# Two columns of padding between blocks of 128 activations, and weight tiles 64 bytes further on

## The chip, the cores and the metric

The kernel runs on one core of a Trainium2 chip. The metric is device time in microseconds (us) of one execution. Engines are named as in the profile: PE is the matrix engine's matmuls, PEld its weight loads, DVE, ACT and POOL the vector, scalar and general engines, SP the queue that issues most DMAs. On-chip memory (SBUF) has 128 partitions; an address below is a byte address within a partition, and every tile stands at the same address in all partitions.

## The reference

Two layers of a decoder trunk on 256 tokens and 2048 features in float32, batch 1. Layer 0 is a gated linear recurrence (HGRN2), layer 1 a sparse attention with compressed, selected and windowed keys (NSA). Each layer projects its input with one wide matrix, mixes along the tokens, gates, projects back and normalizes:

```
q, f_logit, v, z = split(x @ w_in, 4)                      # layer 0: 2048 -> 8192
o = recurrence(q, f_logit, v); o = rms(o) * g_norm * silu(z)
h = LayerNorm(alpha * x + o @ w_out)
q, k_c, v_c, k_s, v_s, k_w, v_w, gate, z = split(h @ w_in) # layer 1: 2048 -> 7216
o = gate0*compressed + gate1*selected + gate2*windowed; o = o * silu(z)
y = LayerNorm(alpha * h + o @ w_out)
```

The matrices hold about 42 million numbers, and all of them are read once; the products with them are most of the matmuls.

## The kernel before

**Precision.** Matmul operands are of the type fp32r, a rounded float32. To keep accuracy each operand is split into a rounded part and the rest (`split`, lines 86 and 87: ACT writes the high part, DVE the low part), and each product is three matmuls: high by high, high by low, low by high.

**Activations** lie in SBUF as a `Pair`: for each group of 4 feature blocks (KG = 4 groups) a tile `hi` and a tile `lo` of 128 partitions x (4 feature blocks, 256 tokens), 4096 bytes a partition. Pair "a" is the input of a layer (tiles `ah`, `al`), Pair "b" the mixer's output (`bh`, `bl`). They come from the pool `acts`, four slots for each of the four names. `put` writes one block of 128 tokens, `at(k, c)` gives the columns c of feature block k. Each 128 x 128 block is 512 bytes a partition.

**Weights** come in tiles of 256 rows by 512 columns (`wr`, loaded by SP on line 113), are split into `wh` and `wl`, and used at once. The pool `wts` has 5 slots of each part, and a pool `wide` gives three more during layer 0.

**Two forms of the projection.** `project` (lines 153 to 155, through `tok_step`) keeps one activation block of 128 tokens stationary in the array and streams 512 weight columns: the moving operand is the weights, 512 columns a matmul (280 in the two calls that take the gate along). In order of k and then of the token tile t, three matmuls follow one another for each block. `project_t` (lines 208, 210, 211) keeps 128 weight columns stationary and streams the 256 tokens: the moving operand is the activations, 256 columns a matmul, and 12 matmuls follow for each k. `project_by_tile` is `project` one token tile after the other; the last projection's weights lie in tiles of their own (pool `late`, `summed`), so that sums of some columns can stand beside them.

**Other matmuls** are the recurrence's (lines 409 to 479), the attention's (lines 571 to 573, 796 to 813), transposes (221) and the compression of keys and values (621 and 622), where the stationary operand is a 122-column slice of `flat` (488 bytes from one slice to the next) and the moving one 256 columns of a weight tile.

**Order.** A planner orders each engine's instructions at build time; on the chip each engine follows its own list and waits on semaphores. Loads of weights are queued on SP and wait for a free slot.

**Addresses.** Pools with `side="right"` grow down from the top of SBUF, the others up from the bottom. `room(p, n)` takes n bytes to move what follows. In this kernel every block of `ah`, `al`, `bh` and `bl` begins at an address that is 64 modulo 512, and every weight slice at 320 modulo 512 (in the last projection some slices at 64). The slices of `flat` begin at all 64 multiples of 8 modulo 512.

Of the kernel before, what the change touches and what calls it, by code (L numbers as in the profile page):

```python
# [9 lines left out]
F32R = mybir.dt.float32r  # L10
# [8 lines left out]
S = 256  # L19
NT = S // 128  # L20
KT = D // 128
KG = KT // 4
# [33 lines left out]
def trunk(ctx, tc, a, out):  # L56
# [6 lines left out]
    consts = ctx.enter_context(tc.tile_pool(name="consts", bufs=1))  # L63
    acts = ctx.enter_context(tc.tile_pool(name="acts", bufs=4))


    def room(p, n):

        p.tile([128, n // 4], F32, name=f"room{n}")

    room(ctx.enter_context(tc.tile_pool(name="edge", bufs=1, side="right")), 160)
    wts = ctx.enter_context(tc.tile_pool(name="wts", bufs=5, side="right"))
    pj = ctx.enter_context(tc.tile_pool(name="pj", bufs=4, space=PSUM))
    mx = ctx.enter_context(tc.tile_pool(name="mx", bufs=4, space=PSUM))
# [3 lines left out]
    def pjb(shape):  # L78
        return pj.tile(shape, F32, name="pjb", tag="pjb")

    def mxb(shape):
        return mx.tile(shape, F32, name="mxb", tag="mxb")

    def split(hi, lo, src):

        act.activation(hi, src, AF.Copy)  # L86
        dve.tensor_tensor(lo, src, hi.bitcast(F32), op=OP.subtract)  # L87
# [8 lines left out]
    class Pair:  # L96


        def __init__(self, name):
            self.hi = [acts.tile([128, 4, S], F32R, name=name + "h") for _ in range(KG)]  # L100
            self.lo = [acts.tile([128, 4, S], F32R, name=name + "l") for _ in range(KG)]

        def put(self, g, t, src):
            c = slice(128 * t, 128 * (t + 1))
            split(self.hi[g][:, :, c], self.lo[g][:, :, c], src)

        def at(self, k, c):
            return self.hi[k // 4][:, k % 4, c], self.lo[k // 4][:, k % 4, c]

    def load(w, j, c0, n):  # L110

# [4 lines left out]
    def weights(w, j, c0, n):  # L116
        return parts(load(w, j, c0, n))
# [16 lines left out]
    def slot(shape, dtype, name, n, more):  # L134

        turn[name] = i = (turn.get(name, -1) + 1) % (n + more)
        p, b = (extra[0], more) if extra[0] and i >= n else (wts, n)
        if spare[0] and name == "wr" and extra[0] is None:

            spare[1] = i = (spare[1] + 1) % (n + SPARE)  # L140
            p, name, b = (spare[0], "ws", SPARE) if i >= n else (wts, name, n)
        return p.tile(shape, dtype, name=name, tag=name, bufs=b)
# [6 lines left out]
        return hi, lo  # L149

    def tok_step(ps, xs, k, t, wh, wl):
        xh, xl = xs.at(k, slice(128 * t, 128 * (t + 1)))
        pe.matmul(ps, xh, wh, start=(k == 0), stop=False)  # L153
        pe.matmul(ps, xh, wl, start=False, stop=False)  # L154
        pe.matmul(ps, xl, wh, start=False, stop=(k == KT - 1))  # L155

    def project(xs, w, c0, also=None, n=512):

        ps = [pjb([128, n]) for _ in range(NT)]
        for j in range(KT // 2):  # L160
            hi, lo = weights(w, j, c0, n)
            for kk in range(2):
                for t in range(NT):
                    tok_step(ps[t], xs, 2 * j + kk, t, hi[:, kk], lo[:, kk])
            if also:
                also(j)
        return ps
# [28 lines left out]
    def project_t(xs, w, c0, before=None, also=None):  # L196

        ps = [pjb([128, 2, S]) for _ in range(2)]
        for j in range(KT // 2):
            hi, lo = before(j) if before else weights(w, j, c0, 512)  # L200
            for kk in range(2):
                k = 2 * j + kk
                xh, xl = xs.at(k, slice(0, S))
                for b in range(4):
                    o = ps[b // 2][:, b % 2]
                    c = slice(128 * b, 128 * (b + 1))

                    pe.matmul(o, hi[:, kk, c], xh, start=(k == 0 and b % 2 == 0), stop=False,  # L208
                              skip_group_check=True)
                    pe.matmul(o, hi[:, kk, c], xl, start=False, stop=False, skip_group_check=True)  # L210
                    pe.matmul(o, lo[:, kk, c], xh, start=False, stop=(k == KT - 1),  # L211
                              skip_group_check=True)
            if also:
                also(j)
        return ps
# [122 lines left out]
    with tc.tile_pool(name="start", bufs=4) as start:  # L338

        idle = start.tile([128, 128], F32, name="idle", bufs=1)  # L340
        dve.memset(idle, 0.0)
        ps = mxb([128, 128])
        for _ in range(WARM):
            pe.matmul(ps, idle, idle, start=True, stop=True)
        loaded = {}

        def fetch(j):
            xr = start.tile([128, 2, S], F32, name="xr")
            raw = slot([128, 2, 512], F32, "wr", 3, 1)
            for c in (slice(0, 1), slice(1, 2)) if j < 2 else (slice(0, 2),):  # L350
                nc.sync.dma_start(xr[:, c], xt[:, 2 * j:2 * j + 2][:, c])
                nc.sync.dma_start(raw[:, c], w0[256 * j:256 * (j + 1), D:D + 512].rearrange(
                    "(k p) n -> p k n", p=128)[:, c])
            loaded[j] = xr, raw

        def before(j):
            if j == 0:
                fetch(0)
                fetch(1)
            if j + 2 < KT // 2:  # L360
                fetch(j + 2)
            xr, raw = loaded.pop(j)
            hi, lo = slot([128, 2, 512], F32R, "wh", 5, 3), slot([128, 2, 512], F32R, "wl", 5, 3)
            xh, xl = (v[j // 2][:, 2 * (j % 2):2 * (j % 2) + 2] for v in (xT.hi, xT.lo))
            for c in (slice(0, 1), slice(1, 2)) if j < 2 else (slice(0, 2),):
                split(xh[:, c], xl[:, c], xr[:, c])
                split(hi[:, c], lo[:, c], raw[:, c])
            return hi, lo

        forget = project_t(xT, w0, D, before=before)  # L370

    with tc.tile_pool(name="setup", bufs=1) as setup:
# [119 lines left out]
    with tc.tile_pool(name="m0", bufs=1) as m0:  # L492
        ad = m0.tile([128, NT, 4, 128], F32, name="ad")
        pool.memset(ad, 0.0)
        for g in range(4):
# [5 lines left out]
            v = m0.tile([128, NT, 512], F32, name="v")  # L501
# [25 lines left out]
    with tc.tile_pool(name="n0", bufs=2) as n0:  # L527
        hb = n0.tile([128, NT, D], F32, name="hb", bufs=1)
        stats = n0.tile([128, NT, 4, 6], F32, name="stats", bufs=1)
        for c in range(4):  # L530
            cs = slice(512 * c, 512 * (c + 1))
            xr = n0.tile([128, NT, 512], F32, name="xr")
# [33 lines left out]
    def split2(pair, at, src):  # L566
        split(pair[0][at], pair[1][at], src)
# [77 lines left out]
    with tc.tile_pool(name="cmp", bufs=1) as cp:  # L645
# [57 lines left out]
        h = ck.hidden()  # L703
        ps = mxb([128, 4, NB])
# [9 lines left out]
        n = (512 + 48) // 2  # L714
        for t, ps in enumerate(project(hT, w1, C_VW, step, n=n)):
            split2(vals, (slice(None), t, 1, slice(0, n)), ps)
        h = cv.hidden()
# [5 lines left out]
        ps = mxb([128, 4, 128])  # L723
# [4 lines left out]
        ps = ps.rearrange("p g d -> p (g d)")  # L728
        for i in range(2):
            r, o = (slice(64 * b, 64 * b + 64) for b in (i, 1 - i))  # L730
            l = slice(64 * i + 32, 64 * i + 64)
# [9 lines left out]
    at = attention.enter_context(tc.tile_pool(name="at", bufs=2))  # L741
# [77 lines left out]
    def query(g):  # L819
        pq = project(hT, w1, C_Q + 512 * g)  # L820
        q = [rotary(at, t, pq[t]) for t in range(NT)]
        ps = [scores(g, t, q[t]) for t in range(NT)]
        return [values(g, t, ps[t]) for t in range(NT)]
# [41 lines left out]
    def summed(raw):  # L865


        parts = [late.tile([128, 2, 576], F32R, name=name) for name in ("wh", "wl")]
        ws = n1.tile([128, 2], F32, name="ws")
        with tc.high_priority(AHEAD):  # L870
            split(*(bass.AP(tensor=v.tensor, offset=v.offset, ap=[v.ap[0], [576, 2], [320, 2], [1, 256]])
                    for v in parts), raw.rearrange("p k (u n) -> p k u n", u=2))
            dve.tensor_reduce(ws, raw[:, :, 256:512], axis=AX.X, op=OP.add)
            split(*(v[:, :, 256:258] for v in parts), ws[:, :, None].to_broadcast([128, 2, 2]))

        def halves(v, kk):
            return bass.AP(tensor=v.tensor, offset=v.offset + 576 * kk, ap=[v.ap[0], [320, 2], [1, 256]])

        return [[halves(v, kk) for v in parts] + [v[:, kk, 0:258] for v in parts] +
                [v[:, kk, 320:576] for v in parts] for kk in range(2)]  # L880

    for c in range(4):
        cs = slice(512 * c, 512 * (c + 1))

        xr = []
# [51 lines left out]
        if c < 3:  # L937
            for t, ps in enumerate(project(oT, a["l1_w_out"], 512 * c, behind)):
                residual(t, ps)
            if c == 2:  # L940
                last_xr = fetch(3)
            if c == 1:
                late = ctx.enter_context(tc.tile_pool(name="late", bufs=8, side="right"))
                g1, b1 = row("l1_ln_g"), row("l1_ln_b")
        else:
            xr.append(last_xr)
            project_by_tile(oT, a["l1_w_out"], 512 * c, finish, summed=summed)
# [33 lines left out]
```

## Time and profile before

| | |
|---|---|
| median of 3 runs | 999.18 us (998.26 to 1000.69) |
| the profiled execution's own time | 999.29 us |
| its span, first to last instruction | 997.6 us |
| PE busy | 981.8 us (98%), 6041 matmuls |
| DVE, ACT, POOL busy | 683.2, 545.4, 116.2 us |
| mean granted PE clock | 0.995 of 2.4 GHz |

A matmul's duration in the profile is its way through the array, and matmuls overlap; what they cost in a stream is the time from one start to the next. That is called the spacing below, and is read from the timeline (starts in us) or from a window's count.

### The profile page before, as it was taken

The numbers are of one execution on the slowest core, as the hardware profiler recorded it, in microseconds if no ns is written. First come the engines' busy times: TensorE is split into PE (matmuls) and PEld (weight loads), VectorE is DVE, ScalarE is ACT, GpSimd is POOL, SyncE is SP. The second block draws the span as 40 slices with busy tenths as digits, with TensorE's granted clock in tenths as the row PEclk, the third lists the DMA queues.
The fourth block names the chain that finished last, engine by engine and source line by source line (L and its number), as shares of the span: only waits on it lengthen the run. The fifth ranks groups of instructions, "written<-read, shape, count | busy, mean of one in ns | idle before, by whom it ended". The sixth has DMA issues, their size and how long they took to land.

```text
span 997.6 us, 15935 instructions
## 1 busy us (share of the span) xinstructions
PE 981.8 (98%) x6041; PEld 882.6 (88%) x6041; DVE 683.2 (68%) x1123; ACT 545.4 (55%) x872; POOL 116.2 (12%) x180
## 2 busy tenths in 40 slices
PE   9999999999999999999999999999999999998996
PEld 8988998899889988888889888999989889986885
DVE  6796668666775677646576756555858568786677
ACT  6654455445544554434476655555857667765340
POOL 0400300030002000310011020101020022042200
PEclk9999999999999999999999999999999999999998
DMA  9775466556555565558467776566454455486662
GB/s 306 258 228 165 150 182 175 167 156 186 173 168 160 173 182 160 167 167 273 147 232 226 244 229 213 174 211 189 125 170 128 148 151 164 151 240 204 202 199 84
DMA packets 101068, 185.25 MB, mean 186 GB/s; under 512 B 6128, under 2 KB 20544, under 8 KB 100736
## 3 DMA queue, kind: packets, MB, share of 16 engines
q1 hardware_dynamic: 99520, 178.67, 57.6%
q0 software_dynamic: 1472, 5.56, 1.7%
q8 instruction: 47, 0.77, 0.3%
q14 instruction: 29, 0.24, 0.1%
HBM read 180.02 MB, written 4.19 MB: 185 GB/s over the span
## 4 chain that ended last, share of the span: by engine, by line
PE 87%; DVE 5%; DMA 4%; ACT 2%; issue 1%; SPq 1%; POOL 0%; DVEq 0%; ACTq 0%; POOLq 0%
PE pjb L154 16%; PE pjb L155 16%; PE pjb L153 16%; PE pjb L208 9%; PE pjb L211 9%; PE pjb L210 9%; DMA wr<-in_l_w_out_dram 3%; DVE wl L87 3%; PE mxb L448 2%; PE mxb L221 1%; ACT wh L86 1%; PE mxb L571 1%; PE mxb L572 1%; PE mxb L573 1%; PE mxb L804 1%
## 5 line engine op out<-in xcount | busy, mean ns | idle before, releaser
L87 DVE TENSOR_TENSOR wl<-wr,wh 128x1024 fp32r<-128x1024 f32 (+2 forms) x305 | 372.0, 1225 | 180.4 <-ACT wh L86 178.8
L86 ACT ACTIVATE wh<-wr 128x1024 fp32r<-128x1024 f32 (+2 forms) x305 | 316.9, 1044 | 304.8 <-PE pjb L155 152.9
L208 PE MATMUL pjb<-ah,wh 128*128 128x256 f32 x832 | 236.8, 285 | 0.5 <-ACT wh L86 0.5
L210 PE MATMUL pjb<-al,wh 128*128 128x256 f32 x832 | 236.2, 285 | 0.0
L211 PE MATMUL pjb<-ah,wl 128*128 128x256 f32 x832 | 235.3, 285 | 0.5 <-DVE wl L87 0.5
L154 PE MATMUL pjb<-wl,ah 128*128 128x512 f32 (+1 forms) x576 | 219.4, 381 | 0.0
L153 PE MATMUL pjb<-wh,ah 128*128 128x512 f32 (+1 forms) x576 | 219.0, 381 | 0.0
L155 PE MATMUL pjb<-wh,al 128*128 128x512 f32 (+1 forms) x576 | 218.9, 380 | 0.0
L208 PEld LDWEIGHTS pjb<-ah,wh 128*128 128x128 f32 x832 | 159.4, 192 | 1.3 <-ACT wh L86 0.9
L211 PEld LDWEIGHTS pjb<-ah,wl 128*128 128x128 f32 x832 | 158.9, 192 | 1.0 <-DVE wl L87 0.9
L210 PEld LDWEIGHTS pjb<-al,wh 128*128 128x128 f32 x832 | 159.3, 192 | 0.4
L155 PEld LDWEIGHTS pjb<-wh,al 128*128 128x128 f32 x576 | 108.3, 188 | 19.6
L153 PEld LDWEIGHTS pjb<-wh,ah 128*128 128x128 f32 x576 | 108.2, 188 | 19.3
L154 PEld LDWEIGHTS pjb<-wl,ah 128*128 128x128 f32 x576 | 108.3, 188 | 18.7
L154 PE MATMUL pjb<-wl,bh 128*128 128x512 f32 (+2 forms) x272 | 103.7, 381 | 1.1 <-DVE wl L87 1.1
L153 PE MATMUL pjb<-wh,bh 128*128 128x512 f32 (+2 forms) x272 | 103.5, 381 | 1.0 <-ACT wh L86 1.0
L155 PE MATMUL pjb<-wh,bl 128*128 128x512 f32 (+2 forms) x272 | 103.4, 380 | 0.0
L154 PEld LDWEIGHTS pjb<-wl,bh 128*128 128x128 f32 x272 | 51.6, 190 | 11.0 <-DVE wl L87 1.7
L153 PEld LDWEIGHTS pjb<-wh,bh 128*128 128x128 f32 x272 | 51.6, 190 | 10.9 <-ACT wh L86 1.4
L155 PEld LDWEIGHTS pjb<-wh,bl 128*128 128x128 f32 x272 | 51.6, 190 | 9.5
L511 POOL TENSOR_TENSOR gz<-gz,gn 128x512 f32<-128x512 f32 x8 | 13.6, 1700 | 312.3 <-ACT gz L510 311.7
L87 DVE TENSOR_TENSOR wl<-ws,wh 128x1024 fp32r<-128x1024 f32 (+2 forms) x33 | 28.2, 863 | 18.4 <-ACT wh L86 18.3
(229 smaller groups left out, 1060.5 us busy)
## 6 DMA issues: line engine op xcount, KB each, us to landing
wr<-in_l_w_in_dram SPq DMA_DIRECT2D x218, 512.0 KB, 3.8
wr<-in_l_w_out_dram SPq DMA_DIRECT2D x64, 512.0 KB, 4.5
ws<-in_l_w_in_dram SPq DMA_DIRECT2D x12, 512.0 KB, 4.5
wr<-in_l_cmp_w_k_dram SPq DMA_DIRECT2D x5, 512.0 KB, 3.9
wr<-in_l_cmp_w_v_dram SPq DMA_DIRECT2D x5, 512.0 KB, 3.8
wr<-in_l_w_in_dram SPq DMA_DIRECT2D x9, 280.0 KB, 3.2
xr<-in_x_dram POOLq DMA_DIRECT2D x4, 512.0 KB, 5.7
norm<-hb POOLq DMA_DIRECT2D x2, 1024.0 KB, 5.7
```

Source lines behind the costliest of these rows:

```text
L86: act.activation(hi, src, AF.Copy)
L87: dve.tensor_tensor(lo, src, hi.bitcast(F32), op=OP.subtract)
L153: pe.matmul(ps, xh, wh, start=(k == 0), stop=False)
L154: pe.matmul(ps, xh, wl, start=False, stop=False)
L155: pe.matmul(ps, xl, wh, start=False, stop=(k == KT - 1))
L208: pe.matmul(o, hi[:, kk, c], xh, start=(k == 0 and b % 2 == 0), stop=False, skip_group_check=True)
L210: pe.matmul(o, hi[:, kk, c], xl, start=False, stop=False, skip_group_check=True)
L211: pe.matmul(o, lo[:, kk, c], xh, start=False, stop=(k == KT - 1), skip_group_check=True)
L221: last[0] = pe.transpose(ps[:, i], src[:, i], ident).ins
L448: pe.matmul(ps[:, h], km[:, h].rearrange("p b r j -> p (b r j)"), later, start=True, stop=True)
L511: pool.tensor_tensor(z, z, gn, op=OP.mult)
L571: pe.matmul(o, a[0], b[0], start=start, stop=False)
```

## The change

Each activation tile becomes one row of 1040 numbers (4160 bytes) a partition, seen as 4 feature blocks by 2 token blocks of 130 columns, of which 128 are used: `hi[g][:, k, t]` is now addressed by block t instead of by columns. Blocks follow one another at 520 bytes. With i = 2k + t counting the 32 blocks of an operand, high parts begin at 64 + 8i modulo 512 and low parts at 320 + 8i. `project_t` streams two pieces of 128 columns that are 8 bytes apart, and its output is seen in two pieces of 128 columns, at the same places as before. `put` and the first split write the same numbers to the new places. The room at the right edge is 64 bytes less, so weight tiles and the tiles below them move up by 64 bytes: weight slices begin at 384 modulo 512. The tiles of the last projection shrink from 576 to 544 columns a row (the second half begins at column 288 instead of 320); the pool `acts` grows by 1024 bytes a partition and `late` shrinks by 4096.

```diff
-    room(ctx.enter_context(tc.tile_pool(name="edge", bufs=1, side="right")), 160)
+    room(ctx.enter_context(tc.tile_pool(name="edge", bufs=1, side="right")), 96)
...
         def __init__(self, name):
-            self.hi = [acts.tile([128, 4, S], F32R, name=name + "h") for _ in range(KG)]
-            self.lo = [acts.tile([128, 4, S], F32R, name=name + "l") for _ in range(KG)]
+            self.hi, self.lo = ([acts.tile([128, 1040], F32R, name=name + n).rearrange(
+                "p (k t n) -> p k t n", k=4, t=NT)[:, :, :, 0:128] for _ in range(KG)] for n in "hl")
 
         def put(self, g, t, src):
-            c = slice(128 * t, 128 * (t + 1))
-            split(self.hi[g][:, :, c], self.lo[g][:, :, c], src)
-
-        def at(self, k, c):
-            return self.hi[k // 4][:, k % 4, c], self.lo[k // 4][:, k % 4, c]
+            split(self.hi[g][:, :, t], self.lo[g][:, :, t], src)
+
+        def at(self, k, t):
+            return self.hi[k // 4][:, k % 4, t], self.lo[k // 4][:, k % 4, t]
...
     def tok_step(ps, xs, k, t, wh, wl):
-        xh, xl = xs.at(k, slice(128 * t, 128 * (t + 1)))
+        xh, xl = xs.at(k, t)
...
-                xh, xl = xs.at(k, slice(0, S))
+                xh, xl = xs.at(k, slice(0, NT))
                 for b in range(4):
-                    o = ps[b // 2][:, b % 2]
+                    o = ps[b // 2][:, b % 2].rearrange("p (t s) -> p t s", t=NT)
...
-                split(xh[:, c], xl[:, c], xr[:, c])
+                split(xh[:, c], xl[:, c], xr[:, c].rearrange("p k (t s) -> p k t s", t=NT))
...
-        parts = [late.tile([128, 2, 576], F32R, name=name) for name in ("wh", "wl")]
+        parts = [late.tile([128, 2, 544], F32R, name=name) for name in ("wh", "wl")]
...
-            split(*(bass.AP(tensor=v.tensor, offset=v.offset, ap=[v.ap[0], [576, 2], [320, 2], [1, 256]])
+            split(*(bass.AP(tensor=v.tensor, offset=v.offset, ap=[v.ap[0], [544, 2], [288, 2], [1, 256]])
...
-            return bass.AP(tensor=v.tensor, offset=v.offset + 576 * kk, ap=[v.ap[0], [320, 2], [1, 256]])
+            return bass.AP(tensor=v.tensor, offset=v.offset + 544 * kk, ap=[v.ap[0], [288, 2], [1, 256]])
 
         return [[halves(v, kk) for v in parts] + [v[:, kk, 0:258] for v in parts] +
-                [v[:, kk, 320:576] for v in parts] for kk in range(2)]
+                [v[:, kk, 288:544] for v in parts] for kk in range(2)]
```

## Rows read from the trace of the kernel before

**Rows 1.** The page: busy time by engine, and the chain that ended last, by engine.

```profile
PE 981.8 (98%) x6041; PEld 882.6 (88%) x6041; DVE 683.2 (68%) x1123; ACT 545.4 (55%) x872; POOL 116.2 (12%) x180
...
PE 87%; DVE 5%; DMA 4%; ACT 2%; issue 1%; SPq 1%; POOL 0%; DVEq 0%; ACTq 0%; POOLq 0%
```

**Rows 2.** Busy time by stretch: start, end, length, then engines, clock, DMA.

```profile
core 0: us, PE busy (x) PEld busy (x) DVE busy (x) ACT busy (x) POOL busy (x), PEclk, DMA share, GB/s
0.00:30.00 30.00, 27.86 (x203) 27.11 (x204) 19.50 (x26) 18.85 (x26) 7.44 (x20) 1.00 0.90 305
30.00:880.00 850.00, 850.00 (x5315) 768.00 (x5314) 578.14 (x964) 480.29 (x779) 85.99 (x146) 1.00 0.59 182
880.00:997.60 117.60, 103.94 (x528) 87.53 (x526) 85.58 (x134) 46.24 (x69) 22.82 (x16) 0.95 0.56 183
```

**Rows 3.** Groups by line and shape in 30 to 880 us.

```profile
L208 PE MATMUL pjb<-ah,wh 128*128 128x256 f32 x754 | 214.7, 285 | 0.0
...
L154 PE MATMUL pjb<-wl,ah 128*128 128x512 f32 x512 | 200.6, 392 | 0.0
...
L154 PE MATMUL pjb<-wl,bh 128*128 128x512 f32 x128 | 50.0, 391 | 0.0
```

**Rows 4.** Busy time of two short stretches, inside one form each.

```profile
127.00:154.00 27.00, 27.00 (x227) 27.00 (x226) 16.53 (x25) 13.26 (x16) 0.00 (x0) 1.00 0.64 186
445.00:493.00 48.00, 48.00 (x213) 39.74 (x213) 27.57 (x34) 15.81 (x17) 2.02 (x3) 1.00 0.63 207
```

**Rows 5.** Timeline of PE, first and last starts of those two streams.

```profile
127.04 0.28 PE L211 MATMUL pjb<-ah,wl 128*128 128x256 f32 x1
...
154.76 0.28 PE L211 MATMUL pjb<-ah,wl 128*128 128x256 f32 x1
...
444.59 0.39 PE L154 MATMUL pjb<-wl,bh 128*128 128x512 f32 x1
...
493.10 0.40 PE L155 MATMUL pjb<-wh,bl 128*128 128x512 f32 x1
```

**Rows 6.** Timeline of PE around a compression step, 593 to 599 us.

```profile
593.45 0.28 PE L621 MATMUL mxb<-wh,flat 128*122 128x256 f32 x1
...
594.38 0.39 PE L153 MATMUL pjb<-wh,ah 128*128 128x512 f32 x1
594.62 0.40 PE L154 MATMUL pjb<-wl,ah 128*128 128x512 f32 x1
...
596.47 0.39 PE L153 MATMUL pjb<-wh,ah 128*128 128x512 f32 x1
...
598.51 0.39 PE L153 MATMUL pjb<-wh,ah 128*128 128x512 f32 x1
```

**Rows 7.** Timeline of PE around the next compression step.

```profile
599.87 0.28 PE L621 MATMUL mxb<-wh,flat 128*122 128x256 f32 x1
...
600.81 0.40 PE L153 MATMUL pjb<-wh,ah 128*128 128x512 f32 x1
...
602.20 0.39 PE L153 MATMUL pjb<-wh,ah 128*128 128x512 f32 x1
```

**Rows 8.** Instructions on tile flat: duration min/median/max, first and last start.

```profile
L621 PE MATMUL mxb<-wh,flat x64: 274/280/291, 540.4 to 636.9; 128*122 128x256 f32 x64
L622 PE MATMUL mxb<-wl,flat x64: 276/280/293, 540.6 to 637.0; 128*122 128x256 f32 x64
```

**Rows 9.** Groups by line and shape: the attention's values, and splits into activations.

```profile
L572 PE MATMUL mxb<-pt,vals 128*128 128x512 f32 x24 | 9.5, 396 | 0.0
...
L87 DVE TENSOR_TENSOR al<-h,ah 128x512 fp32r<-128x512 f32 x8 | 5.5, 690 | 3.1 <-ACT ah L86 3.1
...
L87 DVE TENSOR_TENSOR al<-xr,ah 128x512 fp32r<-128x512 f32 x6 | 4.1, 687 | 0.3 <-ACT ah L86 0.3
```

**Rows 10.** Waits of the SP queue: us in total, times, longest.

```profile
SPq L113 <- DVE wl L87: 575.0, 233, 11.0
```

**Rows 11.** The chain that ended last, in 880 to 997.6 us, by line.

```profile
by line: DMA wr<-in_l_w_out_dram 28.7%; DVE wl L87 17.7%; issue 6.5%; ACT wh L86 5.5%; PE pjb L154 5.2%; PE pjb L155 4.9%; PE pjb L153 4.3%; DMA gb<-in_l_ln_g_dram 4.0%; DVE hb L896 3.3%; DVE stats L898 2.3%; POOL xr L856 2.2%; DVE hb L908 
```

## The prediction

> **What bounds the kernel now.** The page comes first: PE is busy 98% of the span, and 87% of the chain that ended last is PE [rows 1]. The windows say where that holds. From 30 to 880 us PE is busy without a break; in the first 30 us the DMA share is 0.90 and PE has gaps, and after 880 us it has gaps again [rows 2]. There the chain goes through loads of the output matrix (28.7%) and splits on DVE (17.7%) more than through PE [rows 11]. So the pace of the matmuls sets the end for 850 us and hardly counts in the other 148. In those 850 us nothing else is late: the weight queue mostly waits for a free slot, that is for older weights to be used (575.0 us in 233 waits) [rows 10], and the clock is at its upper level throughout (2.4 GHz, 1.00) [rows 2].
>
> PE's busy time says nothing about pace, because matmuls overlap: 285 ns is the way of one 256-column matmul through the array [rows 3]. The spacing is what counts. In a long stretch of `project_t`, 27.00 us hold 225 starts (227 less two in flight at its beginning): 120.0 ns each [rows 4]. In a long stretch of `project`, 214 spacings take 48.51 us: 226.7 ns [rows 5]. Their difference, 106.7 ns for 256 more columns, is 0.417 ns a column. So of both spacings 13.3 ns is no column's time. That is all that a better layout could win for a matmul of these forms.
>
> **Is that spacing a property of the shape, or of the layout?** Rows 6 and 7 answer. The matmuls of lines 621 and 622 stream 256 columns as `project_t` does, but their stationary block moves by 488 bytes each time. Eight spacings take 0.93 us (116.3 ns) in one step [rows 6] and 0.94 us (117.5 ns) in the next [rows 7]; the 112 spacings between two of them that stand next to each other average 117.7 ns; the group's first and last stand in [rows 8]. Right after such a step the 512-column matmuls are slower: nine spacings in 2.09 us (232.2 ns), then nine in 2.04 us (226.7 ns) [rows 6]; in the other step six in 1.39 us (231.7 ns) [rows 7]. I read this as settling. With all operands at the same place modulo 256, the stream of matmuls falls after some 6 to 10 of them into a repeating pattern, 120.0 ns at 256 columns and 226.7 ns at 512. Before it has settled, the short matmul is a little quicker than that (117.7) and the long one a little slower (232). The attention's 512-column matmuls, which come in threes and seldom settle, agree: the 61 spacings behind them that no wait lengthens average 232.6 ns; one of their three lines stands in [rows 9].
>
> **The change part by part.** It removes and adds no instruction and no byte of traffic.
>
> *The short matmuls.* In the stretch that counts, lines 208, 210 and 211 have 754 instructions each [rows 3]. Of the 2,260 spacings 2,213 are not stretched by another kind of matmul in between; they average 119.8 ns. After the change their moving blocks and stationary weights stand at all distances that are multiples of 8 bytes, as the slices of `flat` do now. The nearest price is therefore 117.6 ns (between 117.5 for the attention's 256-column matmuls on keys and 117.7 on `flat`, which has 122 stationary columns instead of 128): -2.2 ns x 2,213 = -4.9 us. The other bound is zero, if the pattern settles within the 12 matmuls that share one activation address.
>
> *The long matmuls.* Lines 153 to 155 have 512 + 128 = 640 instructions each of 512 columns there [rows 3]: 1,920 spacings, of which 1,883 are undisturbed, at 227.6 ns on average, so most are settled. After the change the stationary block moves 8 bytes after every three matmuls. Settling took 6 to 9 matmuls [rows 6, 7], so three don't suffice, and I price them unsettled: 232.0 ns (15 spacings in 3.48 us) [rows 6, 7]. +4.4 ns x 1,883 = +8.3 us. No row shows a 512-column matmul with a stationary block off the 64-byte grid. The bounds are +7.0 us (231.3 ns, the mean of all 431 unsettled ones) and, from the side of `flat`, a gain: if these too lost what the short ones lose, see below.
>
> *The rest.* The 280-column calls never settle now (128.1 ns where 130 would be the settled form), so +0. Weights, keys and values move by 64 bytes: still on the grid of today's blocks, +0. Splits into activations: those that write 128-column pieces today take 690 ns, those that write 256-column runs 687 ns [rows 9], so shorter runs cost nothing, and DVE and ACT are busy 68% and 57% of the 850 us [rows 2]. The last projection's narrower tiles and the first 30 us lie where loads end last [rows 2, 11]: +0. The freed and added memory moves no load, as the slots are as many as before.
>
> *The sum.* -4.9 + 8.3 = +3.4 us. The profiled execution took 999.29 us (span 997.6 and 1.7 around it), within 0.1 us of the median. 999.29 + 3.4 = 1002.7 us.
>
> [...] The same 512-column matmul, on the same tiles and with the same neighbours, runs at 232.2 and then at 226.7 ns [rows 6]. [...] No row here streams a block that begins off the 16-byte grid. [...]
>
> **The rivals.**
>
> *Both forms gain (faster).* The long matmul might behave at mixed distances as the short one does. On `flat` and on keys 117.6 - 106.7 = 10.9 ns of each spacing is left over instead of 13.3. With the same remainder a 512-column matmul takes 213.3 + 10.9 = 224.2 ns: -3.4 x 1,883 = -6.4 us, with the short ones' -4.9 together -11.3: 988.0 us. For it: mixed distances are exactly what changes, and the slow 232 ns were all read at unmixed ones. Against it: the attention's long matmuls stand at another distance in part and are slow too. The place where it decides is the long spacing: below 227.6 + 4.9 / 1.883 = 230.2 ns the change wins. Its far end is the whole remainder gone (119.8 - 106.7 = 13.1 and 227.6 - 213.3 = 14.3 ns), 13.1 x 2,213 + 14.3 x 1,883 = 56 us: 943 us.
>
> *The pattern holds (no change).* If the stream settles on whatever addresses it gets, both forms keep 120.0 and 226.7 ns: 999.3 us. For it: in the last projection the moving operand alternates between 64 and 320 modulo 512, and the spacing stays 226.7. Against it: `flat` never settles.
>
> [...]
>
> **How the numbers follow.** A difference under 0.3% (3 us) can't be told from no change here. The forecast (short ones gain, long ones lose) has a chance of 0.45; its own range is 1001 to 1008.7 (the long ones at 231.3 to 232.6, the short ones at -5.1 to 0). Of it 0.20 falls within 3 us and 0.25 above. Both forms gain: 0.38, of which 0.04 is for the far end; all of it faster. The pattern holds: 0.08, same. Off the grid: 0.09, slower. So faster 0.38, same 0.28, slower 0.34. The range of 984 to 1010 leaves out the far end, a tenth of the gains beyond 984 and about half of the last case, under 0.15 together.
>
> **What would show it.** Step one: in `project_t` windows the count gives 117 to 118 ns instead of 120.0. Step two: in `project` windows 231 to 233 ns instead of 226.7, with no run of equal spacings. Step three: PE still without a break from 30 to 880 us, the waits of SP on freed slots as long as now, and the last 118 us unchanged. The prediction is wrong if the long spacing comes out under 230 ns, if the short one rises above 120, or if the planner, which sees other access patterns, orders the work otherwise.

## The result, and the profile after

The changed kernel takes 1009.68 us (1008.51 to 1010.65, 4 runs) where the kernel before takes 999.3 us (998.26 to 1000.69, 4 runs): a ratio of 1.0103, 95% interval 1.0088 to 1.0118. It is slower by 1.0%, or 10.4 us; the forecast was 1002.7, in a range of 984 to 1010.

The page of the changed kernel, its busy times and its chain; then its windows (columns as in [rows 2]):

```profile
PE 992.6 (98%) x6041; PEld 882.9 (88%) x6041; DVE 682.1 (68%) x1123; ACT 545.0 (54%) x872; POOL 116.7 (12%) x180
...
PE 88%; DMA 5%; DVE 2%; POOL 2%; ACT 1%; issue 1%; SPq 0%; DVEq 0%; POOLq 0%; ACTq 0%
```

```profile
0.00:30.00 30.00, 27.04 (x200) 25.86 (x201) 19.59 (x26) 18.60 (x26) 7.08 (x17) 1.00 0.90 296
30.00:880.00 850.00, 850.00 (x5235) 759.72 (x5234) 569.53 (x936) 472.80 (x757) 83.37 (x146) 1.00 0.59 179
880.00:1008.10 128.10, 115.52 (x610) 97.32 (x608) 93.03 (x162) 53.56 (x92) 26.30 (x18) 0.96 0.58 186
```

The instructions are as many as before on every engine. From 30 to 880 us PE is again without a break, but starts 5235 matmuls instead of 5315 [rows 2]. The 80 that are missing there, and two or three from before, are done after 880 us (610 for 528 [rows 2]), which is why the last stretch is 10.5 us longer. So the time went into the pace of the stream, not into waits. SP's queue confirms it: its waits for freed slots are about as long as in [rows 10].

```profile
SPq L112 <- DVE wl L86: 582.1, 234, 11.4
```

Two groups of the lines by shape, and the splits into activations, which now write pieces of 128 columns (line numbers are one less than before):

```profile
L207 PE MATMUL pjb<-ah,wh 128*128 128x256 f32 x735 | 209.0, 284 | 0.0
...
L153 PE MATMUL pjb<-wl,ah 128*128 128x512 f32 x512 | 202.8, 396 | 0.0
```

```profile
L86 DVE TENSOR_TENSOR al<-h,ah 128x512 fp32r<-128x512 f32 x8 | 5.5, 689 | 3.2 <-ACT ah L85 3.2
```

The durations of single matmuls hardly move (284 and 396 for 285 and 392 ns in [rows 3]) and the split costs 689 ns for 690 [rows 9]. The spacing has to be read from starts. The timeline of the changed kernel, first and last of a `project_t` stream (207 spacings) and of a `project` stream (191):

```profile
129.09 0.28 PE L209 MATMUL pjb<-al,wh 128*128 128x256 f32 x1
...
153.93 0.28 PE L209 MATMUL pjb<-al,wh 128*128 128x256 f32 x1
...
447.43 0.40 PE L152 MATMUL pjb<-wh,bh 128*128 128x512 f32 x1
...
491.80 0.40 PE L152 MATMUL pjb<-wh,bh 128*128 128x512 f32 x1
```

24.84 us in 207 spacings are 120.0 ns, as before [rows 5]. 44.37 us in 191 are 232.3 ns, against 226.7 [rows 5]. Over all undisturbed spacings from 30 to 880 us the 512-column matmul went from 227.65 to 232.21 ns, the 256-column one from 119.77 to 119.95. Summed over the whole run with the disturbed ones, the 512-column spacings take 10.0 us more (522.25 to 532.21) and the 256-column ones 0.85 us more (305.65 to 306.50): about all of the 10.5 us by which the span grew (997.6 to 1008.1). Before, the short stream is one spacing over and over and the long one goes round in threes (226, 227, 227); in the changed kernel neither shows such a pattern. The first 24 spacings of the short stream before [rows 5] and of the one after, in ns, worked out from the starts:

```
before  120 120 120 120 120 120 120 120 120 120 120 120 120 120 120 120 120 120 120 120 120 120 120 120
after   118 119 120 125 115 119 114 119 114 119 115 118 114 120 120 120 124 116 120 120 124 116 120 118
```

The mean is the same, but it comes about in another way, as the experiments show.

### The profile page after: what moved, and what is told of

It reads as the page before. It is cut to its first block, busy times and chain, and to the rows that moved or that the text cites. A ratio compares the mean times of both kernels' runs of the same rounds, so it can differ in the third digit from the quotient of the medians.

```text
span 1008.1 us, 15935 instructions
## 1 busy us (share of the span) xinstructions
PE 992.6 (98%) x6041; PEld 882.9 (88%) x6041; DVE 682.1 (68%) x1123; ACT 545.0 (54%) x872; POOL 116.7 (12%) x180
## 4 chain that ended last, share of the span: by engine, by line
PE 88%; DMA 5%; DVE 2%; POOL 2%; ACT 1%; issue 1%; SPq 0%; DVEq 0%; POOLq 0%; ACTq 0%
PE pjb L153 16%; PE pjb L154 16%; PE pjb L152 16%; PE pjb L207 9%; PE pjb L210 9%; PE pjb L209 9%; DMA wr<-in_l_w_out_dram 2%; PE mxb L447 2%; DMA gb<-in_l_ln_g_dram 2%; PE mxb L220 1%; DVE wl L86 1%; POOL xr L855 1%; PE mxb L570 1%; PE mxb L572 1%; PE mxb L571 1%; POOL xr L854 1%
## 5 line engine op out<-in xcount | busy, mean ns | idle before, releaser
L154 PE MATMUL pjb<-wh,al 128*128 128x512 f32 (+1 forms) x576 | 221.3, 384 | 0.0
L154 PEld LDWEIGHTS pjb<-wh,bl 128*128 128x128 f32 x272 | 51.5, 189 | 10.4
```

## The experiments

In what follows the *distance* is the address of the stationary block less that of the moving one, in bytes modulo 256. The prediction's reading, that a stream settles to 226.7 and 120.0 ns wherever its operands stay at one place, is called the settling theory. The distance theory says that the distance itself sets the pace. Before the change the distance is 0 in both forms (64 and 320). All means of whole kernels below are of undisturbed spacings (those that no other kind of matmul lengthens) from 30 to 880 us, some 1,883 of 512 columns and 2,150 to 2,250 of 256.

### The weights' move alone: w384_only

```diff
-    room(ctx.enter_context(tc.tile_pool(name="edge", bufs=1, side="right")), 160)
+    room(ctx.enter_context(tc.tile_pool(name="edge", bufs=1, side="right")), 96)
```

> The kernel before with its weight tiles 64 bytes further on and nothing else: activations stay at 64 modulo 512, every distance is fixed and on the 64-byte grid. Settling theory (a long matmul is quick only when it meets the same places for some ten matmuls in a row): still settles, 512-column spacing 226 to 228 ns and 996 to 1003 us. Distance theory (only a distance of 0 modulo 256 between weights and activations gives 226.7): about 232 ns and 1007 to 1010 us. Grid theory (what costs is a block that doesn't begin on a 64-byte or 16-byte boundary): 226.7 ns, 999 us.

Measured: 994.25 us (990.59 to 997.86, 10 runs), 0.9950 of before, 0.9934 to 0.9966. The move of the weights by itself is a gain; the loss comes from the padding. The distance is now 192 in `project` and 64 in `project_t`; the spacings are 229.65 ns (+2.0) and 116.52 ns (-3.25): +3.8 and -7.2 us. Both streams still repeat, only not at the old pace, so a fixed place does not by itself lead to 226.7 and 120.0: the settling theory is wrong. The distance theory as expected here (0 alone is quick, about 232 ns and 1007 to 1010 us) is not right either, nor is the grid theory's 226.7 ns; that each distance has a pace of its own came out of the table below. The timeline of this kernel, first and last of three streams of 210, 58 and 220 spacings:

```profile
125.73 0.28 PE L208 MATMUL pjb<-ah,wh 128*128 128x256 f32 x1
...
150.46 0.28 PE L208 MATMUL pjb<-ah,wh 128*128 128x256 f32 x1
...
531.88 0.28 PE L210 MATMUL pjb<-al,wh 128*128 128x256 f32 x1
...
538.46 0.28 PE L211 MATMUL pjb<-ah,wl 128*128 128x256 f32 x1
...
440.70 0.39 PE L154 MATMUL pjb<-wl,bh 128*128 128x512 f32 x1
...
491.05 0.39 PE L153 MATMUL pjb<-wh,bh 128*128 128x512 f32 x1
```

24.73 / 210 = 117.8 ns, 6.58 / 58 = 113.4 ns, 50.35 / 220 = 228.9 ns. The first two are the same instructions at the same distance, and differ by 4.3 ns. The last experiment comes back to that.

### Padding on the 16-byte grid: pad_k

```diff
-                "p (k t n) -> p k t n", k=4, t=NT)[:, :, :, 0:128] for _ in range(KG)] for n in "hl")
+                "p (k n) -> p k n", k=4)[:, :, 0:256].rearrange("p k (t n) -> p k t n", t=NT) for _ in range(KG)] for n in "hl")
```

The padded tile of the changed kernel, but with four spare columns behind each pair of token blocks in place of two behind each block, so that the moving operand is one piece and begins on a multiple of 16 bytes.

> The changed kernel with the four padding columns behind each pair of token blocks instead of two behind each block: 256 tokens are one piece again, and blocks begin on the 16-byte grid; the stationary place moves by 16 bytes after six matmuls instead of by 8 after three. Settling theory: six matmuls settle only at times, 512-column spacing 229 to 232 ns, 1004 to 1009 us. [...] Theory that the two-piece moving operand keeps the short matmul at 120: it falls to 117.6, and the time by 5 us against the changed kernel.

Measured: 1004.26 us (1002.25 to 1006.87, 6 runs), 1.0059 of before, 1.0037 to 1.0081. The long spacing is 232.12 ns, as in the changed kernel, so the grid theory's 226.7 ns and 999 us fall for a grid of 16 bytes too; the settling theory's 229 to 232 ns is just missed. The short spacing is 118.26 instead of 119.95 ns, and the time is 5.1 us above before instead of 10.4, much as the theory of the two-piece operand expected. The first and last of one of its `project_t` streams, 219 spacings apart (118.4 ns):

```profile
126.69 0.28 PE L207 MATMUL pjb<-ah,wh 128*128 128x256 f32 x1
...
152.62 0.28 PE L207 MATMUL pjb<-ah,wh 128*128 128x256 f32 x1
```

So most of the forecast gain on short matmuls does exist at mixed distances. In `project_t` the first 128 columns stand at the same sixteen distances in both kernels (both advance by 1040 bytes a feature block); what differs is that the changed kernel's second piece begins 8 bytes off a multiple of 16. It also makes two pieces of the operand. That a break alone costs nothing can be read for 512 columns from the kernel before: 48 matmuls of its last projection stream two pieces of 256 columns, both on multiples of 16 bytes, and 47 undisturbed spacings average 227.1 ns, where one piece has 226.7 [rows 5]. For 256 columns no run has two pieces that both begin on a multiple of 16.

### The spacing by distance: map_fixed and map_steps

Both compute no layer, and each ran once. `map_fixed` has 24 matmuls at each of 64 places, 8 bytes apart, three times: 512 columns with the stationary block moved, then 256 columns with the stationary block moved, then 256 columns with the moving block moved. `map_steps` moves a block on after every so many matmuls.

```diff
+    for d in range(64):
+        for i in range(24):
+            pe.matmul(ps, A[:, 2 * d:2 * d + 128], B[:, 0:512], start=(i == 0), stop=(i == 23))
...
+    for w in (1, 2, 4, 8, 16, 64):
+        for m in (1, 3, 6, 12, 24):
+            for i in range(96):
+                c = 2 * w * (i // m) % 1024
+                pe.matmul(ps, A[:, c:c + 128], B[:, 0:512], start=(i == 0), stop=(i == 95))
```

> No layer is computed: 24 matmuls at each of 64 stationary places 8 bytes apart, with 512 and with 256 moving columns, then 256 columns at 64 moving places; the output is a part of the input and one product. Settling theory: within 24 matmuls most places reach a repeating spacing, for 512 columns near 226.7 ns on the grid and off it. Grid theory: 226.7 at places that are multiples of 64 (or 16) bytes, 232 at the others. Distance theory: 226.7 at distances 0 and 256 alone.

> No layer is computed: 96 matmuls of 512 columns for each step of the stationary place (8, 16, 32, 64, 128 and 512 bytes) after each number of matmuls (1, 3, 6, 12, 24); then 256 columns whose moving place steps by 16 bytes after 1, 3 or 12, in one piece and in two. Settling theory: 231 to 233 ns at 1 and 3 matmuls for every step but 512 bytes, falling to under 229 at 24, and 226.7 for 512 bytes throughout. Grid theory: steps of 64 and 128 bytes stay at 226.7, steps of 8 to 32 stand near 232 whatever the number of matmuls. For the short matmul: two pieces cost under 1 ns more than one if the gap itself is free, some 3 ns if it explains why the changed kernel's short matmuls stand at 120.

Means from `map_fixed` in ns, of each place's spacings but the first two, for the first place at each distance. In the last row the moving block is moved, by 256 bytes less the distance:

```
distance                         0     32     64     96    128    160    192    224 | all 64 places
512 columns, stationary moved  226.7  233.4  233.5  234.3  232.4  233.3  228.9  233.2 | 231.9
256 columns, stationary moved  120.0  118.3  113.3  117.4  120.0  119.8  117.8  116.5 | 118.3
256 columns, moving moved      119.4  118.2  114.0  117.4  118.7  119.9  117.8  117.0 | 119.0
```

Five of these cells in the timeline, the first three 512 columns at 0, 64 and 192, then 256 columns at 0 and 64 with the stationary block moved. Each line runs to the end of its last matmul, which is 0.39 or 0.28 us on its way; without that, 23 spacings give 227.0, 233.5, 229.1, 120.0 and 113.9 ns, the first two spacings of each place included:

```profile
19.11 5.61 PE L75 MATMUL ps<-B,A 128*128 128x512 f32 x24
63.61 5.76 PE L75 MATMUL ps<-B,A 128*128 128x512 f32 x24
152.87 5.66 PE L75 MATMUL ps<-B,A 128*128 128x512 f32 x24
...
375.45 3.04 PE L78 MATMUL ps<-B,A 128*128 128x256 f32 x24
398.24 2.90 PE L78 MATMUL ps<-B,A 128*128 128x256 f32 x24
```

Places 256 bytes apart agree, to 0.1 ns in nearly every pair (the worst, 256 columns at distance 0, by 0.7). For 512 columns only the distances 0 and 120 (not in the table; the distance theory expected 0 alone) give 226.7 ns; 192 and 240 give 228 to 229, and all others 230 to 234. So, by this table, the kernel before stood at the best place for its long matmuls and at one of the worst for its short ones. The mean over all places, 231.9 and 118.3 ns, is what a layout gets that runs through them: pad_k has 232.12 and 118.26. With the moving block moved, the even multiples of 8 bytes average 117.96 ns and the odd ones 119.99; with the stationary block moved both average 118.29. Thus about 2 ns is the mean price of a moving block that begins off the 16-byte grid, in one piece as well, and the stationary block pays nothing for it. The distance does not settle everything: at 144, with both blocks on the 16-byte grid, the spacing is 120.0 ns with the stationary block moved and 115.4 with the moving one moved. No run shows whether the place itself counts there, or what ran before.

`map_steps`, 512 columns: with the block moved by 8 bytes after every 1, 3, 6, 12 and 24 matmuls the mean is 231.5, 232.45, 232.4, 231.9 and 230.4 ns. Steps of 16 to 128 bytes lie between 230.3 and 234.1, and steps of 512 bytes keep 226.67 throughout. If streams settled in 6 to 10 matmuls at any place, 24 would have come to under 229 ns, as that theory expected; it is 230.4, close to the mean of the table's four distances that it visits (230.2). Steps of 64 and 128 bytes stay on the 64-byte grid and are slow as well, so for the stationary block the grid is no cause either. The 256-column stream of two pieces with 8 bytes between them (a loop that is not in the extract) takes 119.6 to 120.2 ns, that of one piece 117.4 to 118.2.

### Other fixed distances: w448, w256 and acts32

The kernel before with its weights at 448 (room 32) or 256 (room 224) modulo 512, or with its activations 32 bytes further on:

```diff
-    room(ctx.enter_context(tc.tile_pool(name="edge", bufs=1, side="right")), 160)
+    room(ctx.enter_context(tc.tile_pool(name="edge", bufs=1, side="right")), 32)
```

```diff
+    ctx.enter_context(tc.tile_pool(name="left", bufs=1)).tile([128, 8], F32, name="left32")
```

> The kernel before, weights at 448 modulo 512: stationary and moving blocks stand at a fixed distance of 128 modulo 256 in both forms. Distance theory, with the table of fixed places: 512 columns 232.4 ns (227.65 before, +4.75 x 1,883 = +8.9 us), 256 columns 118.7 to 120.2 ns (119.8 before, -2.4 to +0.9 us): 1006 to 1009 us. Rival, any fixed place on the 64-byte grid settles to 226.7 and 120.0 ns: 999 us.

> The kernel before, weights at 256 modulo 512: distance from moving to stationary block 64 modulo 256 in project and 192 in project_t. Distance theory: 512 columns 233.4 ns (+5.75 x 1,883 = +10.8 us), 256 columns 117.7 ns (-2.1 x 2,213 = -4.6 us): 1005.5 us. Rival, any fixed place on the 64-byte grid settles: 999 us.

> The kernel before, activations 32 bytes further on (96 modulo 512, weights still at 320): distance 32 modulo 256 in project and 224 in project_t. Distance theory: 512 columns 233.4 ns (+10.8 us), 256 columns 116.7 to 118.4 ns (-6.9 to -3.0 us): 1003 to 1007 us. Rival, any fixed place settles: 999 us.

| | distances, long and short | 512 columns | 256 columns | measured | ratio to before, 95% |
|---|---|---|---|---|---|
| w448 | 128, 128 | 232.71 | 118.77 | 1007.54 us | 1.0089 (1.0074 to 1.0104) |
| w256 | 64, 192 | 233.20 | 117.52 | 1004.34 us | 1.0053 (1.0037 to 1.0068) |
| acts32 | 32, 224 | 233.22 | 117.18 | 1003.40 us | 1.0049 (1.0032 to 1.0066) |

All three times lie within 1.2 us of what was worked out from the table, and none at 999 us. From the spacings w256 should lose 5.55 x 1,883 - 2.25 x 2,213 = 5.5 us, and does lose 5.4 (before on that chip: 998.97). The timeline of w448, first and last of a short stream (217 spacings, 118.7 ns) and of a long one (196, 233.4 ns):

```profile
126.78 0.28 PE L211 MATMUL pjb<-ah,wl 128*128 128x256 f32 x1
...
152.54 0.28 PE L208 MATMUL pjb<-ah,wh 128*128 128x256 f32 x1
...
445.61 0.40 PE L153 MATMUL pjb<-wh,bh 128*128 128x512 f32 x1
...
491.35 0.40 PE L155 MATMUL pjb<-wh,bl 128*128 128x512 f32 x1
```

### The order of the matmuls: map_order

Again only matmuls, run once, at eight distances and in three orders, the last of them the kernel's own. An extract:

```diff
+    for d in range(0, 256, 32):
...
+                u, v = (i // 3, i % 3) if order else (0, 0)
+                b = u % 6 if order == 2 else 0
+                o = two[u % 2] if order == 2 else ps
+                cs, cm = 128 * b + s + 1024 * (v == 2), 1024 * (v == 1)
```

> No layer is computed: only matmuls, 48 in each stretch, with the stationary block at eight distances from the moving one (32 bytes apart), in three orders: always the same two blocks; the kernel's three matmuls (high by high, high by low, low by high) on one pair of blocks; the same with the block moving by 512 bytes after every three and the output alternating as in the kernel. If only the distance modulo 256 counts, the three orders agree at each distance (512 columns: 226.7 ns at 0, 228.9 at 192, 232.4 to 234 at the six others; 256 columns: 113.3 at 64, 120.0 at 0). If the order has a part in it, the third order differs at 64 with 256 columns (116.5 as in the kernel with weights alone moved, where the table said 113.3), and at 0 as well if the kernel's 226.7 is the order's.

The three orders agree within 0.3 ns at each of the eight distances and in both forms. At 0 the 226.7 and 120.0 ns are there with one pair of blocks repeated as well as in the kernel's own order. So at these distances neither the alternation of high and low parts nor that of outputs has a part in it. But three of the sixteen cells are over 1 ns from the table: 256 columns at 96 and 128 (118.6 and 118.7 for 117.4 and 120.0), and above all 512 columns at 192, which run at 233.3 ns in all three orders where `map_fixed` and w384_only had 228.9. And 256 columns at 64 run at 113.3, not at w384_only's 116.5. The first of the three stretches of 512 columns at 192 (47 spacings, 233.2 ns without the last matmul's 0.40 us):

```profile
321.61 11.36 PE L82 MATMUL ps<-B,A 128*128 128x512 f32 x48
```

### The padded kernel with its weights elsewhere: after_w448

```diff
-    room(ctx.enter_context(tc.tile_pool(name="edge", bufs=1, side="right")), 96)
+    room(ctx.enter_context(tc.tile_pool(name="edge", bufs=1, side="right")), 32)
```

> The changed kernel with its weights 64 bytes further on (448 instead of 384 modulo 512). Distance theory: as the padded blocks run through all distances anyway, it is indifferent where the weights begin, and the spacings stay at 232.2 and 120.0 ns: 1009.7 us within 2 us, though the same step of 64 bytes cost the unpadded kernel 13 us (994.3 to 1007.5). Rival, the place of the weights has a price of its own: 1016 us or more.

Measured: 1007.82 us (1006.44 to 1008.95, 4 runs), 1.0095 of before, 1.0066 to 1.0124, which holds the changed kernel's 1.0103. The spacings are 232.25 and 120.01 ns. With padding the place of the weights is indifferent, for the two places tried (384 and 448); without it the same step of 64 bytes moves the time from 994.25 to 1007.54 us.

### What ran before the stream: map_prelude

Six matmuls at another distance (`e`, of `n` columns), then 36 at 192 with 512 columns or at 64 with 256. No layer is computed; it ran once.

```diff
+    for c, d in ((512, 192), (256, 64)):
+        for n in (256, 512):
+            for e in range(0, 256, 32):
+                for i in range(6):
+                    mm(two[1][:, 0:n], e, n, i, 5)
+                for i in range(36):
+                    mm(ps[:, 0:c], d, c, i, 35)
```

> No layer is computed: only matmuls. 36 at a distance of 192 (512 columns) or 64 (256 columns), each time behind six matmuls of 256 or 512 columns at one of eight other distances. Theory that a distance has more than one steady pattern and that what ran before chooses: stretches of 228.9 and others of 233.3 ns, and of 113.3 and others of 117.8 ns, equal from first to last within a stretch. Rival, the second level in the kernel comes from other engines at work: all stretches alike, 113.3 ns for the short ones.

Both levels are there, on a core on which nothing else runs. Of 16 long streams 12 settle at 228.8 to 228.9 ns and 4 at 233.3; of 16 short ones 10 at 113.3 and 6 at 117.8. The four streams shown, as the timeline has them (36 matmuls to the end of the last, in the order of the table below):

```profile
20.23 8.41 PE L76 MATMUL ps<-B,A 128*128 128x512 f32 x36
...
38.29 8.56 PE L76 MATMUL ps<-B,A 128*128 128x512 f32 x36
...
179.24 4.25 PE L76 MATMUL ps<-B,A 128*128 128x256 f32 x36
...
169.52 4.41 PE L76 MATMUL ps<-B,A 128*128 128x256 f32 x36
```

Their first nine spacings, from the starts in the trace, and the mean of the last twelve:

```
512 columns at 192, behind six of 256 columns at   0: 226 229 232 226 229 232 225 230 231 ... 228.9
512 columns at 192, behind six of 256 columns at  64: 232 233 233 234 233 233 234 233 233 ... 233.3
256 columns at  64, behind six of 256 columns at  64: 114 113 113 114 113 113 114 113 113 ... 113.3
256 columns at  64, behind six of 256 columns at   0: 118 117 118 118 117 119 117 118 118 ... 117.8
```

A distance can thus have two patterns, each of which repeats to the end of the stream. So 228.9 and 233.3 ns at 192 need not contradict each other, and other engines at work are not needed for the second level. What ran before has a part in the choice, but the six matmuls before the stream do not decide it alone: behind six of 256 columns at 160 the long stream took 228.8 ns here, behind the 48 of `map_order` 233.3. It accounts for w384_only's 116.5 ns as well: of its 52 stretches of 18 to 48 short matmuls 20 run at 113 to 115 ns and 32 at 117.8; of its 51 long ones 47 run at 229 to 230 and 4 at 233. Those four begin at 52.5, 152.9, 253.4 and 353.8 us, the same point of four equal rounds, which speaks against chance.

## Why the prediction was right or wrong

**The sign and the size of the long term: right.** The measured 1009.7 us lies in the range of 984 to 1010, at its upper end. The forecast time was slower, as it came, though its chances put faster (0.38) above slower (0.34). The long term was put at +4.4 ns x 1,883 = +8.3 us. It came to +4.56 x 1,883 = +8.6 us, inside its bounds. PE stayed without a break and SP's waits stayed as long; splits, loads and the first 30 us cost about nothing, as forecast.

**Where it failed: the short matmuls.** The step "The nearest price is therefore 117.6 ns" gave -4.9 us; the spacing went to 119.95 ns, +0.4 us, and the first of the prediction's signs, 117 to 118 ns in `project_t`, did not show (120.0). It is a term with the wrong size, and its mechanism was half right. Mixed distances do win, 119.77 to 118.26 ns in pad_k, or 1.5 x 2,213 = 3.3 us. But the price was read where no moving block leaves the 16-byte grid (on `flat` [rows 8] it is the stationary block that does), and was carried over to a moving block that leaves it. For the second piece of the moving block that costs 119.95 - 118.26 = 1.7 ns, and the gain is gone. The prediction left 0.09 for such a price ("Off the grid"); no row of before shows one, so that chance, and about half of it above the range, were the author's estimate. `map_fixed` puts the price at 2.0 ns on the mean over distances (119.99 for 117.96).

**A smaller miss: the end.** The last projection was put at nothing because loads end last there [rows 11]. Its 512-column spacings went from 227.46 to 232.50 ns, 1.2 us in the sum of all of them after 880 us. Together: 5.3 us of short matmuls, 1.2 us at the end and 0.3 us of long ones are the 7.0 us between 1002.7 and 1009.7, within half a us.

**The reading of the pattern: wrong in form.** "With all operands at the same place modulo 256, the stream of matmuls falls after some 6 to 10 of them into a repeating pattern, 120.0 ns at 256 columns and 226.7 ns at 512" is true of distance 0, where rows 5 to 7 were read. A stream does take a few matmuls to find its pattern (nine at 232.2 ns before the 226.7 in [rows 6]), but the pattern depends on the distance: 230 to 234 ns at nearly all others, to the end of every stream seen. That the long price came out right is luck: the unsettled 232.0 ns [rows 6, 7] happens to be the mean over all distances (231.9). The same error hid the one gain in the diff: the weights' move, which the prediction put at nothing in itself.

**The other rivals.** "Both forms gain" fell: the long spacing decided it at 230.2 ns, and mixed distances have 232.2. One argument against it was misread: by the kernel's own addresses the attention's 72 matmuls of 512 columns all stand at distance 0 (stationary blocks at 0, moving ones at 256 modulo 512), not at another one in part. They come in threes and average 232.6 ns all the same; distance 0 gave 226.7 in longer streams. "The pattern holds" fell with the rows of unequal spacings above. In the table of `map_fixed`, where only the place of one operand against the other changes, the spacings shown spread over 7.6 ns at 512 columns (226.7 to 234.3) and 6.7 ns at 256 (113.3 to 120.0): the shape alone does not set them.

**What the sum by spacings gives.** From the two means alone, against 227.65 and 119.77 ns, w256 comes to +5.5 us (measured +5.4), acts32 to +4.8 (+4.4), pad_k to +5.1 (+5.1), after_w448 to +9.2 (+8.9), w448 to +7.3 (+8.6), w384_only to -3.4 (-4.9), and the changed kernel to +9.0 (+10.4).

**What stays open.** What in the memory or the array makes a distance fast was not found; the runs show that the distance counts, and that at some distances what ran before counts too, but no rule for which pattern is taken. Whether a kernel can be made to take the fast pattern at 64 each time was not tried; from w384_only's rows I estimate (116.5 - 113.3) x 2,213 = 7 us for it. The padded kernel with weights left at 320 was not tried, because the tiles leave no room for it; after_w448 makes a difference there unlikely.

The best version is w384_only: one number changed, 994.25 us.

## What to carry to other kernels

Read the pace of a matmul stream from its starts, and when it is a constant that its columns do not account for (here 226.7 ns, where 512 columns at the 0.417 ns estimated from [rows 4, 5] make 213.3), ask at what distance its two operands stand. Before spreading addresses, price every fixed distance with a table of a few dozen matmuls each: here mixing gave about the mean of the table (pad_k 232.12 and 118.26 ns for 231.9 and 118.3), and one layout of fixed distances (before, 999.3 us) was better than the mixed pad_k (1004.3), another (w384_only, 994.3) was better still, and w448 (1007.5) was worse. Check the choice in the kernel, as one distance can have two paces (228.9 and 233.3 ns at 192). When a price is carried from one operand to the other (stationary to moving), look for a row where that very operand does it.

## What the runs showed of the hardware

- In these fp32r streams the spacing depends on the distance of stationary and moving block modulo 256: 226.7 to 234.3 ns at 512 columns, 113.3 to 121.9 ns at 256 (`map_fixed`, stationary block moved; granted clock 1.00 in both windows read, 19.2 to 24.2 and 153 to 158 us). The forms want different distances: 0 is among the best for 512 columns (226.7) and poor for 256 (120.0); 64 is among the best for 256 (113.3) and poor for 512 (233.5). At distance 0, 256 more columns take 106.7 ns, 0.417 ns each on the mean at a granted clock of 1.00 [rows 2, 4, 5], or 2.4 columns a ns; the prediction's 2.4 GHz has no other row behind it.
- At some distances there are two lasting patterns (228.9 and 233.3 ns at 192 with 512 columns; 113.3 and 117.8 ns at 64 with 256). What ran before has a part in which one is taken; the rule is not known.
- A moving block that begins at an odd multiple of 8 bytes costs about 2 ns a matmul on the mean over distances (`map_fixed`, 256 columns: 119.99 for 117.96 ns at even ones); a stationary block does not (118.29 for both).
